# Delta head 0's three projection tiles and the gates' product on x*(1+scale), block by block, with W*shift added later

## The chip, the cores and the metric

The kernel runs on one core of a Trainium2 chip. The metric is the device time of one launch in microseconds (us); the median of 3 runs before the change is 921.39 us (920.76 to 921.51).

## What is computed

One inference step of a decoder layer, on 512 prompt tokens and 8 x 4 sample tokens (544 columns), all in float32:

```
shift, scale, gate = split(silu(c) @ w_cond + b_cond)     # 9 rows of c: one prompt, eight samples
h = x * (1 + scale) + shift
qa, ka, va, za, qkv_b, zb, a_b, b_b, g_a, g_b = h @ w_in  # 11,280 columns
branch A: dilated window attention, 24 heads of 64, with caches for the samples
branch B: gated DeltaNet, 8 heads of 128: short causal convolution (width 4) and silu on q, k, v,
          gates from a_b and b_b, chunked delta rule, RMSNorm, times silu(zb)
merged = sigmoid(g_a) * (yA @ w_branch_a) + sigmoid(g_b) * (yB @ w_branch_b)
y = LayerNorm(ALPHA * x + gate * (merged @ w_out))
```

The samples' updated caches are outputs too: they are copied from DRAM to DRAM, 512 KB at a time, all through the kernel.

## The kernel before

Everything on the chip is transposed: a tile has 128 features on the partitions and the 544 tokens along the free dimension. A float32 product is made of three products of rounded halves: a weight tile `wt` is split into `hi` (ScalarE copies it to the shorter format) and `lo` (VectorE subtracts), and h into `hhi` and `hlo`, and each of the 8 contraction steps k takes `hi*hhi`, `hi*hlo` and `lo*hhi`. One projection tile (128 output columns of w_in) is thus 2 halves of 272 tokens x 8 steps x 3 = 48 matmuls of 272 columns, written to PSUM tiles `pp`. 88 such tiles follow each other ("the stream"), and beside them run, on TensorE too, the small matmuls of attention (`pg`), of the delta blocks (`pb`) and of the delta rule (`pd`).

The order of instructions on each engine is fixed when the program is built. `body` records every operation with a rank, and `Recorder.schedule` is a list planner with assumed costs: it emits, engine by engine, the operation of lowest rank that it believes ready. All records therefore carry the same source line (L724 before, L723 after), and tiles are told apart by name. Some operations have a planned time (`at`): the cache copies and the loads of the gate third of w_cond.

The front, before the stream can start:

- `cT` (c transposed) is loaded, silu gives `cs`, 8 x 32 columns.
- The scale third of w_cond, then the shift third, come in four pieces `wc` of 1,024 KB each (two k steps, all 1024 columns). `cond_product` multiplies them: 16 matmuls of 32 rows by 512 columns for each third, four of them side by side in the array's four column strips. The four strips are summed and transposed back by eight small matmuls against `selc` (a part of the constants `cst`): `Y` is the copy out of PSUM, `pd<-cst,Y` the matmuls. Out of this come `sc` = 1 + scale and then `sh` = shift.
- `xT` (x transposed, 8 steps of 544 columns, 2.2 MB in all) becomes h: the samples' columns by `xs * sc` and `xs + sh` (VectorE), the prompt's by one `tensor_scalar` with sc and sh for each k (VectorE), then `hhi` (ScalarE) and `hlo` (VectorE) for each k.
- All transfers go through one queue, SyncE's (SPq).

The stream's first three tiles are q, k and v of delta head 0 (`conv_job(0, s)`, s = 1, 0, 2); next come nine attention tiles, six tiles of heads 1 and 2, and so on. A conv tile's `evac` copies PSUM to `ext` (ScalarE), a convolution of four steps follows (`acc`, one on ScalarE and three on VectorE), and silu into `KQ` or `uv`. `gates()` makes a product of 16 columns of w_in (`wab`, as `hl` with both halves in 32 columns) with hhi and hlo: 32 matmuls `pg<-hhi,hi 32x272`; its result `abT` goes through eight small matmuls and some 40 small VectorE operations on 34 columns, to `beta`, `cum` and, by DRAM, `drows`. `delta_blocks(h)` waits for KQ and the gates, transposes (`pb<-cst,KQ`), takes row norms (`rc`), sends them through DRAM (`dr`) and back as a broadcast (`rb`), scales KQ and multiplies (`pb<-KQ`). `gate_rows` makes the gate third, planned for 110 to 200 us.

Of the kernel before, what the change touches and what calls it, by code (L numbers as in the profile page):

```python
# [11 lines left out]
F32 = mybir.dt.float32  # L12
F32R = mybir.dt.float32r
# [232 lines left out]
class Recorder:  # L246
# [208 lines left out]
    def schedule(self):  # L455
# [37 lines left out]
        def ready(op):  # L493
# [283 lines left out]
def body(ctx, tc, io):  # L777
# [98 lines left out]
    wab = consts.tile([128, KT, 16], F32, name="wab")  # L876
    gctx = ExitStack()
    d1 = pool(gctx, "gtab", 1)
    tables["g"] = d1.tile([128, CONST[1].shape[1]], F32, name="cg")
    dta = d1.tile([128, 2, 34], F32, name="dta")  # L880
    with ExitStack() as fctx:
        fr = pool(fctx, "front", 1)
        cT = fr.tile([128, KT, 32], F32, name="cT")
        ve.memset(cT, 0.0)
        sp.dma_start(cT[:, :, 0:9], io["cT"])
        bT = fr.tile([128, 24], F32, name="bT")
        sp.dma_start(bT, io["bT"])
        th = fr.tile([128, KT, 32], F32, name="th")
        se.activation(th, cT, AF.Tanh, scale=0.5)
        ve.tensor_scalar(th, th, 0.5, 0.5, op0=OP.mult, op1=OP.add)  # L890
        ve.tensor_mul(cs, cT, th)
        xT = fr.tile([128, KT, NT], F32, name="xT")
        pieces = {}
        for part in (1, 0):
            for k in range(0, KT, 2):
                pieces[part, k] = fr.tile([128, 2, D], F32, name="wc", bufs=8)
                sp.dma_start(pieces[part, k], cond_rows(part, k, 2))
                if (part, k) == (1, 6):
                    sp.dma_start(cst, io["const"])
        sp.dma_start(wab, io["w_ab"])  # L900
        raws[0] = wraw.tile([128, D], F32, name="wt", tag="wraw")
        sp.dma_start(raws[0], io["w_in"][TILE_AT["b", 0, 1]])
        weights[0] = split(raws[0], D, ve)
        for k in range(0, KT, 2):
            sp.dma_start(xT[:, k:k + 2], io["xT"][:, k:k + 2])
# [4 lines left out]
        def load_front(part):  # L910
            for k in range(0, KT, 2):
                for n in range(2):
                    for q in range(2):
                        yield k + q, n, pieces[part, k][:, q, 512 * n:512 * n + 512]

        sc = fr.tile([128, KT, 9], F32, name="sc")
        sh = fr.tile([128, KT, 9], F32, name="sh")
        for part, t in ((1, sc), (0, sh)):
            ps = [pp(), pp()]
            take(cond_product(part, load_front, ps), 99)  # L920
            pv = f16(pd())
            bias = bT[:, 8 * part:8 * part + 8, None].to_broadcast([128, 8, 9])
            for n in range(2):
                Y = fr.tile([128, 512], F32, name="Y", bufs=2)
                if n:
                    se.activation(Y, ps[n], AF.Copy)
                else:
                    ve.tensor_copy(Y, ps[n])
                to_features(pv, 4 * n, Y)
            if part:  # L930
                ve.scalar_tensor_tensor(t, pv[:, :, 0:9], 1.0, bias, op0=OP.add, op1=OP.add)
            else:
                ve.tensor_add(t, pv[:, :, 0:9], bias)
        sp.dma_start(bnw, io["b_norm_w"])
        ve.tensor_scalar(hbnw, bnw, 0.5, None, op0=OP.mult)
        xs = xT[:, :, SEQ:].rearrange("p k (b t) -> p k b t", t=4)
        per_token = lambda t, k, n: t[:, k:k + n, 1:9, None].to_broadcast([128, n, 8, 4])
        for k in range(0, KT, 2):
            ve.tensor_mul(xs[:, k:k + 2], xs[:, k:k + 2], per_token(sc, k, 2))
        for k in range(0, KT, 2):  # L940
            ve.tensor_add(xs[:, k:k + 2], xs[:, k:k + 2], per_token(sh, k, 2))
        for k in range(KT):
            h = xT[:, k]
            ve.tensor_scalar(h[:, :SEQ], h[:, :SEQ], sc[:, k, 0:1], sh[:, k, 0:1], op0=OP.mult, op1=OP.add)
            se.activation(hhi[:, k, :], h, AF.Copy)
            ve.tensor_sub(hlo[:, k, :], h, hhi[:, k, :].bitcast(F32))
# [65 lines left out]

    two_tiles = lambda t: t[:, 0:512].rearrange("p (s g n) -> p s g n", s=2, g=2)
# [23 lines left out]
    def gates():  # L1037
        d1 = pool(gctx, "gt", 1)


        hl = cols128(wsp.tile([128, D], F32R, name="hi", tag="hi"))
        se.activation(hl[:, :, 0:16], wab, AF.Copy)
        ve.tensor_sub(hl[:, :, 16:32], wab, hl[:, :, 0:16].bitcast(F32))
        ps = [pg(), pg()]
        for n in range(2):
            for k in range(KT):
                for x in (hhi, hlo):
                    pe.matmul(ps[n][0:32, :HF], hl[:, k, 0:32], x[:, k, n * HF:(n + 1) * HF],
# [1318 lines left out]
```

## Time and profile before

| What | Value |
|---|---|
| Median of 3 runs | 921.39 us |
| Time of the profiled execution | 921.47 us |
| Its span, first to last instruction | 919.7 us |
| TensorE (PE) busy | 883.6 us, 96% of the span |
| VectorE (DVE), ScalarE (ACT), GpSimd (POOL) busy | 663.6, 459.5, 68.5 us |
| Moved by DMA | 240.09 MB, mean 261 GB/s |
| Mean granted TensorE clock | 0.987 |

Times in the profile count from the start of the span. A matmul's record includes the time that it takes to drain, so matmuls overlap in the records: what a stream of them costs is read from the distance of their starts, or from how many start in a stretch. A float32 matmul that isn't split by the kernel shows as two records. In the page's row of the granted clock, a digit is tenths of the full clock; the trace has an event only where the clock changes.

### The profile page before, as it was taken

The page shows a single profiled execution, that of the slowest core. Times are in us where ns is not written, and L with a number is a line of the kernel's source. Part 1 is how long each engine was busy: PE and PEld are TensorE (multiplying, and loading weights), DVE is VectorE, ACT ScalarE, POOL GpSimd, SP SyncE. Part 2 cuts the span into 40 slices and gives each one's busy share as a digit, 9 for nine tenths or more (in the row PEclk, how much of TensorE's full clock was granted, in tenths as well). Part 3 has the DMA queues.
Part 4 walks back from the last instruction along what each step waited for, and adds up shares of the span by engine and source line. Part 5 has one row for each costly group of instructions (what it writes and reads, how often), then busy time and mean ns, then how long its engine had stood idle before and what let it go on. Part 6 is the DMA issues. An engine that isn't in the chain of part 4 may idle for free.

```text
span 919.7 us, 20682 instructions
## 1 busy us (share of the span) xinstructions
PE 883.6 (96%) x8082; PEld 823.5 (90%) x8082; DVE 663.6 (72%) x1399; ACT 459.5 (50%) x1115; POOL 68.5 (7%) x186
## 2 busy tenths in 40 slices
PE   4899999999999999999999999999999999989995
PEld 1699998898999999898999989999999999989884
DVE  0574535674568999759999865656889799988578
ACT  0266457663568863577764676554342222224331
POOL 0120000100001200001200010002010000001000
PEclk9899999999999999999999999999999999999998
DMA  9778785765788879896889865648969899985933
GB/s 354 256 186 273 204 286 198 252 215 173 229 265 292 289 219 346 256 288 220 297 269 310 261 207 179 234 149 285 353 197 352 303 380 427 373 308 194 324 118 122
DMA packets 107807, 240.09 MB, mean 261 GB/s; under 512 B 31110, under 2 KB 62480, under 8 KB 105020
## 3 DMA queue, kind: packets, MB, share of 16 engines
q1 hardware_dynamic: 107708, 238.76, 77.4%
q8 instruction: 64, 1.05, 0.5%
q14 instruction: 35, 0.29, 0.1%
HBM read 222.40 MB, written 104.00 MB: 355 GB/s over the span
## 4 chain that ended last, share of the span: by engine, by line
PE 86%; DVE 5%; DMA 4%; ACT 2%; SPq 1%; issue 1%; DVEq 0%; POOL 0%; POOLq 0%; ACTq 0%
PE pp L724 67%; PE pg L724 8%; PE pd L724 7%; PE pb L724 4%; DMA rb<-dr 2%; DMA wc<-in_w_cond 1%; SPq L724 1%; DMA dO<-orow 1%; DVE r L724 1%; DVE acc L724 1%; DVE lo L724 1%; DVE xT L724 0%; ACT sq L724 0%; ACT hi L724 0%; DVE KQ L724 0%
## 5 line engine op out<-in xcount | busy, mean ns | idle before, releaser
L724 PE MATMUL pp<-hhi,hi 128*128 128x272 f32 x1408 | 416.4, 296 | 2.6 <-ACT hhi L724 2.1
L724 PE MATMUL pp<-hhi,lo 128*128 128x272 f32 x1408 | 417.1, 297 | 0.0
L724 PE MATMUL pp<-hlo,hi 128*128 128x272 f32 x1408 | 414.3, 295 | 0.4 <-DVE hlo L724 0.2
L724 PEld LDWEIGHTS pp<-hhi,hi 128*128 128x128 f32 x1408 | 266.7, 190 | 6.8 <-issue 2.9
L724 PEld LDWEIGHTS pp<-hhi,lo 128*128 128x128 f32 x1408 | 266.7, 190 | 3.7 <-issue 2.1
L724 PEld LDWEIGHTS pp<-hlo,hi 128*128 128x128 f32 x1408 | 266.7, 190 | 3.4 <-issue 1.4
L724 ACT ACTIVATE hi<-wt 128x1024 fp32r<-128x1024 f32 (+1 forms) x104 | 106.8, 1026 | 148.6 <-PE pp L724 111.7
L724 DVE TENSOR_TENSOR lo<-wt,hi 128x1024 fp32r<-128x1024 f32 (+1 forms) x104 | 122.6, 1179 | 72.7 <-ACT hi L724 72.3
L724 DVE SCALAR_TENSOR_TENSOR acc<-ext,cw,acc 128x568 f32<-128x568 f32 x72 | 57.4, 797 | 0.7 <-ACT acc L724 0.4
L724 ACT ACT_TABLE_LOAD x36 | 46.2, 1283 | 15.9 <-DMA cT<-in_cT 8.2
L724 DVE TENSOR_TENSOR slab<-slab 128x512 f32<-128x512 f32 (+1 forms) x66 | 42.9, 670 | 1.5 <-DMA slab<-in_ks 0.7
L724 DVE TENSOR_REDUCE slab<-slab 128x8 f32<-128x512 f32 (+2 forms) x66 | 42.5, 660 | 0.3
L724 ACT ACTIVATE zt<-pp 128x272 f32<-128x272 f32 x48 | 18.6, 388 | 42.9 <-PE pp L724 40.6
L724 PE MATMUL pp<-ybl,hi 128*128 128x272 f32 x128 | 36.9, 288 | 0.0
L724 PE MATMUL pp<-ybh,hi 128*128 128x272 f32 x128 | 36.9, 288 | 0.0
L724 PE MATMUL pp<-ybh,lo 128*128 128x272 f32 x128 | 36.9, 288 | 0.0
L724 ACT ACTIVATE P<-P,st 128x256 f32<-128x256 f32 (+1 forms) x64 | 31.3, 491 | 10.0 <-DVE st L724 9.8
L724 DVE CUSTOM_DVE_ANT_0 P<-pg,bias 128x256 f32<-128x256 f32 (+1 forms) x64 | 23.1, 401 | 15.2 <-PE pg L724 15.2
L724 POOL COPY cx<-ext 128x3 f32<-128x3 f32 (+1 forms) x48 | 24.7, 544 | 94.7 <-ACT ext L724 94.7
L724 DVE TENSOR_TENSOR Tb<-Tb,tmp 32x15 f32<-32x15 f32 (+7 forms) x120 | 23.4, 195 | 4.1
L724 ACT ACTIVATE ext<-pp 128x272 f32<-128x272 f32 (+2 forms) x72 | 19.9, 315 | 12.7 <-PE pp L724 12.7
L724 PE MATMUL pp<-wc,cs 128*32 128x512 f32 x64 | 13.7, 984 | 12.7 <-DMA wc<-in_w_cond 12.7
(382 smaller groups left out, 1527.5 us busy)
## 6 DMA issues: line engine op xcount, KB each, us to landing
out_kv_s<-in_cache SPq DMA_DIRECT2D x144, 512.0 KB
wt<-in_w_in SPq DMA_DIRECT2D x88, 512.0 KB
out_kv_s<-in_cache SPq DMA_DIRECT2D x24, 496.0 KB
wc<-in_w_cond SPq DMA_DIRECT2D x8, 1024.0 KB
slab<-in_ks SPq DMA_DIRECT2D x32, 256.0 KB
slab<-in_vs SPq DMA_DIRECT2D x32, 256.0 KB
kv<-in_ks SPq DMA_DIRECT2D x16, 512.0 KB
kv<-in_vs SPq DMA_DIRECT2D x16, 512.0 KB
```

The costliest lines, as they stand in the source:

```text
L724: getattr(real[x.engine], x.name)(*map(arg, x.args), **{k: arg(v) for k, v in x.kw.items()})
```

## The change

- w_cond's scale and shift thirds are laid out anew (`w_cb`): four blocks of 256 columns for each third, all 8 k steps in a block (two transfers of 512 KB). `cond_block` does for one block what the front did for a third: 8 matmuls of 32 x 256, a copy `Y`, two transposing matmuls.
- As soon as block b of scale is there, `x1` = x * sc is made for the two k steps 2b and 2b+1, in halves `x1h` (`x1[0]`, ScalarE) and `x1l` (`x1[1]`, VectorE), and these two steps of head 0's three tiles run on it: six PSUM tiles (`sums`, two each of the pools pp, pd, pg) stay open over all four blocks. Their weights and the gates' 16 columns are one new input, `w3` (tile `W3`, 400 columns, four loads of 410 KB). The gates' product also runs on x1.
- The six sums are copied to `raw` tiles and abT, without the shift. Shift's four blocks follow; then `W3 * sh` (8 matmuls 32 x 400 and four transposing ones) gives `shifts`, which `shifted()` adds (VectorE) when it fills `ext`, in place of ScalarE's evac.
- h itself is made block by block as shift lands; the `tensor_scalar` of odd k moves to GpSimd. The program that is built has one more GpSimd instruction ahead of them (a reload of its code library).
- cg, dta, abT, the raw tiles and the gates' small tiles lie in the nine tiles of the pool `op` (tag "o"), freed when the gates are done; `gate_rows` now waits for `gates_over` first. The gates have rank -2 in place of 2.
- In the planner, an operation waits for the free time of every tile that it touches, not of those alone that it is first to use. With that, rows move by a few places all through the program.

```diff
-                if t.ops[0] == op.n:
-                    r = max(r, t.free + self.WAKE[op.engine])
+                r = max(r, t.free + self.WAKE[op.engine])
...
+        def load_cond(part, b):
+            pieces[part, b] = fr.tile([128, KT, 256], F32, name="wc", bufs=4)
+            for k in (0, 4):
+                sp.dma_start(pieces[part, b][:, k:k + 4], io["w_cb"][part, b, :, k:k + 4])
...
+        for b in range(4):
+            load_cond(1, b)
+            if not b:
+                sp.dma_start(cst, io["const"])
+                sp.dma_start(bT, io["bT"])
+            sp.dma_start(xT[:, 2 * b:2 * b + 2], io["xT"][:, 2 * b:2 * b + 2])
+            sp.dma_start(W3[:, 2 * b:2 * b + 2], io["w3"][:, 2 * b:2 * b + 2])
+        for b in range(4):
+            load_cond(0, b)
+        for i in range(2):
+            raws[i] = wraw.tile([128, D], F32, name="wt", tag="wraw")
+            sp.dma_start(raws[i], io["w_in"][TILE_AT["a", 0, 0, i]])
...
+            with rec.together():
+                for k in range(KT):
+                    q = k % 4
+                    pe.matmul(ps[32 * q:32 * q + 32, 0:256], cs[:, k, :], wc[:, k, :], start=(k < 4), stop=(k >= 4),
+                              tile_position=(0, 32 * q))
+            Y = fr.tile([128, 256], F32, name="Y", bufs=2)
+            ve.tensor_copy(Y, ps[:, 0:256])
...
+            for k in range(2 * b, 2 * b + 2):
+                se.activation(x1[0][:, k, :SEQ], xT[:, k, :SEQ], AF.Copy, scale=sc[:, k, 0:1])
...
+                for t in range(3):
+                    w, w_ = (x[:, k % 2, 128 * t:128 * t + 128] for x in (hi, lo))
+                    for n in range(2):
+                        for a, x in ((w, 0), (w, 1), (w_, 0)):
+                            pe.matmul(sums[t][n], a, x1[x][:, k, cols_of(n)], start=(k == 0 and a is w and x == 0),
+                                      stop=(k == KT - 1 and a is w_))
...
+                pe.matmul(ps[32 * q:32 * q + 32, 0:400], sh[:, k, :], W3[:, k, :], start=(k < 4), stop=(k >= 4),
+                          tile_position=(0, 32 * q))
...
+        for b in range(4):
+            kk = slice(2 * b, 2 * b + 2)
+            ve.tensor_add(xs[:, kk], xs[:, kk], per_token(sh, 2 * b, 2))
+            for k in range(2 * b, 2 * b + 2):
+                h = xT[:, k]
+                (ge if k % 2 else ve).tensor_scalar(h[:, :SEQ], h[:, :SEQ], sc[:, k, 0:1], sh[:, k, 0:1], op0=OP.mult, op1=OP.add)
+                se.activation(hhi[:, k, :], h, AF.Copy)
+                ve.tensor_sub(hlo[:, k, :], h, hhi[:, k, :].bitcast(F32))
...
-    for s in (1, 0, 2):
-        jobs.append(conv_job(0, s))
+    for t, s in enumerate((1, 0, 2)):
+        job = conv_job(0, s)
+        job.begin()
+        job.shifted(first[t], shifts[:, t])
...
-    ab = threads.add(gates(), 2)
-    threads.add(stream(60 + 4 + EARLY_B), 9)
-    threads.run(lambda: ab["over"])
-    gctx.close()
+    threads.add(gates(), -2)
+    threads.add(stream(57 + 4 + EARLY_B), 9)
```

How rows move: a row names engine operation, output tile, input tiles and shape; in these lists the tile `W3` reads W_117 and the copy `Y4` reads Y_578. First TensorE at the start of the program. Before:

```order
L724 MATMUL pp<-wc,cs 32x512 x16
L724 MATMUL pd<-cst,Y 128x9 x8
L724 MATMUL pp<-wc,cs 32x512 x16
L724 MATMUL pd<-cst,Y 128x9 x8
L724 MATMUL pp<-hhi,hi 128x272 x2
```

After the change, TensorE at scale's block 2 (blocks 0 and 1 stand ahead of it in the same way):

```order
L723 MATMUL pg<-x1h,hi 128x272
L723 MATMUL pg<-wc,cs 32x256 x8
L723 MATMUL pg<-x1l,hi 128x272
L723 MATMUL pg<-x1h,lo 128x272
L723 MATMUL pp<-x1h,hi 128x272
L723 MATMUL pp<-x1l,hi 128x272
L723 MATMUL pp<-x1h,lo 128x272
```

Where both thirds of w_cond stood ahead of the first projection matmul, a block's product now stands among the tile matmuls of the blocks before it, and its two transposing matmuls some seven matmuls further on, here behind five on `pp`.

Second, TensorE where the front ends. Before, the gates' product on h begins behind the 42nd matmul of the first tile:

```order
L724 MATMUL pp<-hhi,hi 128x272
L724 MATMUL pp<-hlo,hi 128x272
L724 MATMUL pp<-hhi,lo 128x272
L724 MATMUL pg<-hhi,hi 32x272
L724 MATMUL pg<-hlo,hi 32x272
```

After, behind all 144 tile matmuls, three matmuls of the first attention tile and shift's last block, the gates' product on x1 ends and the shift's product stands inside it; these are its last rows:

```order
L723 MATMUL pg<-x1h,hl 32x272
L723 MATMUL pg<-x1l,hl 32x272
L723 MATMUL pp<-hhi,hi 128x272
L723 MATMUL pb<-cst,Y_578 128x9 x3
L723 MATMUL pb<-cst,Y_578 16x9
L723 MATMUL pp<-hlo,hi 128x272
L723 MATMUL pp<-hhi,lo 128x272
```

The stream on hhi and hlo thus goes on at the first attention tile, with head 0's three tiles and the gates' product behind it.

Third, VectorE at shift. Before (three more rows of the samples' columns and the eight `hlo` follow):

```order
L724 TENSOR_TENSOR sh<-pd,bT 128x72
L724 TENSOR_TENSOR xT<-xT,sh 128x2x32
L724 TENSOR_TENSOR xT<-xT,sc 128x2x32
L724 TENSOR_TENSOR xT<-xT,sh 128x2x32 x2
L724 TENSOR_SCALAR xT<-xT,sc,sh 128x512 x3
```

After, from shift's block 0 into block 1:

```order
L723 TENSOR_TENSOR sh<-pg,bT 128x2x9
L723 TENSOR_TENSOR xT<-xT,sh 128x2x32
L723 TENSOR_SCALAR xT<-xT,sc,sh 128x512
L723 COPY Y<-pb 128x256
L723 TENSOR_TENSOR hlo<-xT,hhi 128x544
L723 TENSOR_TENSOR sh<-pb,bT 128x2x9
L723 TENSOR_TENSOR lo<-wt,hi 128x1024
```

One `sh` for all k steps has become one for two of them, and each block's copy `Y`, for which TensorE waits, stands between subtractions `hlo` of the block before, which wait for ScalarE's hhi and for GpSimd's `tensor_scalar` of the odd k.

More of the change, by code (lines that the diff above doesn't have):

```diff
@@ new lines, in body @@
+    n = CONST[1].shape[1]
+    tables["g"] = early_[:, 0:n]
+    dta = early_[:, n:n + 68].rearrange("p (a b) -> p a b", b=34)
+    shifts = early_[:, n + 68:n + 104].rearrange("p (a b) -> p a b", b=9)
+    first = [op.tile([128, NT], F32, name="raw", tag="o") for _ in range(3)]
+    abT = op.tile([128, NT], F32, name="abT", tag="o")[0:32]
+    xs = xT[:, :, SEQ:].rearrange("p k (b t) -> p k b t", t=4)
+    per_token = lambda t, k, n: t[:, k:k + n, 1:9, None].to_broadcast([128, n, 8, 4])
+    cols_of = lambda n: slice(n * HF, (n + 1) * HF)
@@ L881, in body @@
     with ExitStack() as fctx:
         fr = pool(fctx, "front", 1)
-        cT = fr.tile([128, KT, 32], F32, name="cT")
-        ve.memset(cT, 0.0)
-        sp.dma_start(cT[:, :, 0:9], io["cT"])
+        cT = fr.tile([128, KT, 9], F32, name="cT")
+        sp.dma_start(cT, io["cT"])
         bT = fr.tile([128, 24], F32, name="bT")
[L887 to L890, printed above, removed]
@@ L934, in body @@
-        sp.dma_start(bnw, io["b_norm_w"])
-        ve.tensor_scalar(hbnw, bnw, 0.5, None, op0=OP.mult)
[L936 to L946, printed above, removed]
+        sp.dma_start(bnw, io["b_norm_w"])
@@ new lines, in body, with cond_block @@
+        ve.memset(cs, 0.0)
+        ge.memset(sh, 0.0)
+        th = fr.tile([128, KT, 9], F32, name="th")
+        se.activation(th, cT, AF.Tanh, scale=0.5)
+        ve.tensor_scalar(th, th, 0.5, 0.5, op0=OP.mult, op1=OP.add)
+        ve.tensor_mul(cs[:, :, 0:9], cT, th)
+        def cond_block(part, b):
+            ps, wc = pb_() if b % 2 else pg(), pieces[part, b]
+            rec.rank = -1
+            with rec.together():
[5 more added lines that the diff above has]
+            ve.tensor_copy(Y, ps[:, 0:256])
+            pv = ps[:, 256:288].rearrange("p (a b) -> p a b", b=16)
+            with rec.together():
+                for i in range(2):
+                    pe.matmul(pv[:, i, 0:9], Y[:, 128 * i:128 * i + 128], C("selc"), start=True, stop=True)
+            rec.rank = 0
+            return pv[:, :, 0:9], bT[:, 8 * part + 2 * b:8 * part + 2 * b + 2, None].to_broadcast([128, 2, 9])
@@ new lines, in body @@
+        Y = fx.tile([128, 400], F32, name="Y4")
+        rec.either(Y, ps[:, 0:400])
+        with rec.together():
+            for t in range(4):
+                m = 128 if t < 3 else 16
+                pe.matmul(pv[0:m, 16 * t:16 * t + 9], Y[:, 128 * t:128 * t + m], C("selc"), start=True, stop=True)
+        ve.tensor_copy(shifts[:, 0:3], pv[:, 0:48].rearrange("p (a b) -> p a b", b=16)[:, :, 0:9])
+        ve.tensor_copy(shifts[0:16, 3], pv[0:16, 48:57])
+        ab = abT[0:16]
+        ve.tensor_scalar(ab[:, :SEQ], ab[:, :SEQ], shifts[0:16, 3, 0:1], None, op0=OP.add)
@@ L1037, in gates, with tile @@
     def gates():
[L1038 to L1048, printed above, removed]
-                              start=(k == 0 and x is hhi), stop=(k == KT - 1 and x is hlo))
-        abT = d1.tile([32, NT], F32, name="abT")
-        for n in range(2):
-            se.activation(half(abT, n), ps[n][0:32, :HF], AF.Copy)
-        yield 2.0
+        packs, at = [], [NT]
+        spare_packs = [op.tile([128, NT], F32, name="gt", tag="o") for _ in range(3)]
+        class d1:
+            def tile(shape, dtype, name):
+                n = math.prod(shape[1:])
+                if at[0] + n > NT:
+                    packs.append(spare_packs.pop(0))
+                    at[0] = 0
+                t = packs[-1][0:shape[0], at[0]:at[0] + n]
+                at[0] += n
+                return t if len(shape) == 2 else t.rearrange("p (a b) -> p a b", b=shape[2])
         pa = pg()
```

140 lines of the change are left out of this document (83 added, 57 removed).

## The prediction

> **What bounds the kernel now.** The page first: busy times and the slices.
>
> ```profile
> PE 883.6 (96%) x8082; PEld 823.5 (90%) x8082; DVE 663.6 (72%) x1399; ACT 459.5 (50%) x1115; POOL 68.5 (7%) x186
> PE   4899999999999999999999999999999999989995
> ```
>
> TensorE (PE) is full from the third slice on and loses time only in the first two, 46 us. So I read that stretch next, in windows (after PE come granted clock, DMA share, GB/s):
>
> ```profile
> 10.00:20.00 10.00, 7.35 (x32) 1.00 1.03 407
> 20.00:30.00 10.00, 9.22 (x49) 1.00 1.03 407
> 30.00:40.00 10.00, 6.90 (x41) 0.66 0.92 305
> ...
> 90.00:100.00 10.00, 10.00 (x80) 1.00 0.68 189
> ```
>
> The last row is the steady stream: 80 matmuls in 10 us, 0.125 us each. From 10 to 30 us the DMA engines are full (407 GB/s) and PE does few matmuls. Which, and how fast, the timeline tells:
>
> ```profile
> 8.15 1.28 ACT L724 ACT_TABLE_LOAD   x1 [8.15 <-DMA cT<-in_cT]
> ...
> 10.85 1.93 PE L724 MATMUL pp<-wc,cs 128*32 128x512 f32 x8 [10.85 <-DMA wc<-in_w_cond]
> ...
> 18.45 1.94 PE L724 MATMUL pp<-wc,cs 128*32 128x512 f32 x8 [0.64 <-DMA wc<-in_w_cond]
> 21.16 3.58 PE L724 MATMUL pd<-cst,Y 128*128 128x9 f32 x16 [0.78 <-DVE Y L724]
> 24.68 5.92 PE L724 MATMUL pp<-wc,cs 128*32 128x512 f32 x32
> 31.40 2.39 PE L724 MATMUL pd<-cst,Y 128*128 128x9 f32 x16 [0.80 <-DVE Y L724]
> 35.92 0.82 PE L724 MATMUL pp<-hhi,hi 128*128 128x272 f32 x2 [2.13 <-ACT hhi L724]
> 37.31 0.43 PE L724 MATMUL pp<-hhi,lo 128*128 128x272 f32 x1
> 37.54 0.43 PE L724 MATMUL pp<-hhi,hi 128*128 128x272 f32 x1
> 157.15 1.92 PE L724 MATMUL pd<-wg,cs 128*32 128x512 f32 x16
> ```
>
> The front is two w_cond products, each behind its transfers, and no projection matmul before 35.9. Two more things stand here. The first piece of 1,024 KB is there at 10.85, the fourth at 18.45: 2.53 us each, the pace of the windows' 407 GB/s. And PE ran the front at half speed, whatever the window's clock column says before the first change of the clock: 8 records of the w_cond product took 1.93 us at 10.85, 16 equal ones 1.92 at 157.15; the stream at 37.5 started one matmul every 0.23 us, against 0.125 later. In the row at 24.68 32 records took 5.92 us: at 0.24 and 0.12 us each, the speed changed at about 28.8; the mean clock of 0.66 from 30 to 40 is half clock for 6.8 us of the ten.
>
> **Where the old front ends.** The chain of waits (start, us, what):
>
> ```profile
> 43.86 4.54 PE pg L724 x36
> 48.40 0.95 PE pp L724 x6
> 49.35 0.72 PE pg L724 x12
> 50.07 11.53 PE pp L724 x90
> 61.60 0.79 PE pg L724 x8
> 62.38 0.23 PE pp L724
> 62.61 1.19 PE pg L724 x10
> 63.80 1.46 PE pp L724 x10
> ```
>
> With the 42 tile matmuls ahead of 43.86 (the order above), the 144th of head 0's tiles is done five before the last row's end, at 64.6. In between PE did 32 matmuls of the gates' product and 3.2 us of other gate work (4 of the 36, then 0.72, 0.79, 1.19), which the change leaves behind the front. So before, "both w_cond products, 144 tile matmuls and 32 gate matmuls done" is at 64.6 - 3.2 = 61.4 us. The same point after the change gives the saving, if the stream behind it runs as before.
>
> **The change, part by part.** *Transfers.* At that pace, byte count B (in MB) lands at 18.45 + (B - 5.85)/0.407 us: 5.85 MB (xT's first part, two wt, cT, bT, four wc) are there at 18.45. After, one wt (0.52), cT, then block 0 come first: cT at 5.5 (so the table load, 1.28, ends at 6.8 and `cs` is ready at 7.6), block 0 of scale at 8.1, its x and W3 at 10.9, the next scale blocks at 13.4, 18.4, 23.4, the last W3 at 25.7, shift's blocks at 28.2, 30.8, 34.7 and 39.1. The two wt between them, for the first two attention tiles, land at 32.1 and 36.0, well before their use (51 and 57). Gate tables, passed by all this, land at 36.5; they are used at 54.
>
> *PE until it is fed.* Block 0's product runs at half speed, 8.1 to 10.0 (1.93), copy `Y` 0.4, two transposing matmuls (a quarter of 3.58) to 11.4. Then sc, and x1: W3 lands at 10.9, its `hi` (three quarters of 1.06) ends at 11.85, and the first x1h of 512 columns at about 12.65.
>
> ```profile
> L724 DVE TENSOR_TENSOR lo<-wt,hi 128x1024 fp32r<-128x1024 f32 x11 | 13.5, 1224 | 23.1 <-ACT hi L724 23.0
> L724 DVE TENSOR_TENSOR hlo<-xT,hhi 128x544 fp32r<-128x544 f32 x8 | 5.4, 714 | 0.7 <-ACT hhi L724 0.7
> L724 DVE TENSOR_SCALAR xT<-xT,sc,sh 128x512 f32<-128x512 f32 x8 | 3.9, 536 | 0.0
> L724 DVE COPY Y<-pp 128x512 f32<-128x512 f32 x2 | 1.4, 692 | 10.4 <-PE pp L724 10.4
> ...
> L724 ACT ACTIVATE hi<-wt 128x1024 fp32r<-128x1024 f32 x11 | 11.6, 1058 | 12.6 <-PE pp L724 11.0 <-PE pg L724 1.6
> L724 ACT ACTIVATE hhi<-xT 128x544 fp32r<-128x544 f32 x8 | 4.7, 648 | 6.8 <-DVE xT L724 6.8
> ...
> L724 POOL COPY cx<-ext 128x3 f32<-128x3 f32 x3 | 2.5, 849 | 7.9 <-ACT ext L724 7.9
> ...
> L724 POOL MEMSET XF<- 128x512 f32 x1 | 0.5, 525 | 0.0
> ```
>
> *PE from 12.65 on.* A scale block brings 36 tile matmuls (4.5 us), a product and two transposes, some 6 us; its data take 5 us to land and VectorE 3.5 us to prepare. PE has a backlog from here, so work adds up:
> - 176 tile and gate matmuls x 0.125 = 22.0;
> - 7 products: 16 records of 256 columns, half of 157.15's 1.92, plus 0.15 for the change of shape = 1.1 each, 7.7;
> - 7 pairs of transposes: 4 records, a quarter of 2.39 at most, 0.5 each, 3.5;
> - the shift's product, new: 16 records of 400 columns, 400/512 of 1.92 = 1.5, and 4 transposes, 0.95;
> - half speed at the start. Between 1.7 (half of the 3.4 us that the dense stream from 35.9 ran slowly) and 8.1 (half of 12.65 to 28.8). PE is as dense here as in the stretch from 35.9, the nearest case, but with gaps for block 0's x1l: 2.5;
> - waits: VectorE's `Y` of shift's last block stands behind `lo` of a weight tile (1.22) and hlo; PE reaches its transposes some 0.7 early, and W*shift 0.4 early: 1.1.
>
> Sum: 12.65 + 22.0 + 7.7 + 3.5 + 2.45 + 2.5 + 1.1 = 51.9 us. Saving 61.4 - 51.9 = 9.5 us.
>
> The Trainium skill, TensorE: Matmul & The Clock Gate, Part 1, has half speed end after one busy window of about 3.4 us; the trace agrees (0.23 us at 37.5, full clock 3.4 us behind 35.9). By it the fifth term would be 1.7, and the sum 51.1.
>
> *Work off PE.* h follows shift's blocks: the last `sh` at 47.8, hhi and hlo of k = 7 at 50.7, used behind 20 attention matmuls at about 54: covered by 3 us. GpSimd's `tensor_scalar` has no row; bounds are 0.53 (the memset of equal size) and 1.5 (three of them, since it reads, computes and may share VectorE's time); I take 1.0, nearest the memset. What queues behind it: hlo of odd k on VectorE, then the next block's `Y`, for which PE waits; PE's slack there is 1 us, so the upper end costs 0.5. The reload ahead of it stands on an idle engine at 1 us, first use at 34.6: between 0 and the 1.28 of ScalarE's table load, taken as 0. ScalarE's nine evac copies give way to six `raw` copies; VectorE gains three times one tensor_scalar and an add, 2.3 us, while PE streams.
>
> *Head 0's delta blocks* come later in the stream than before by some 75 matmuls, since ext now waits for `shifts` (51.9); on the clock they stay where they were (transposes at 62, against 65.3). Nothing before h = 1's third tile waits for them. `gate_rows`' wait ends at about 75, its work is planned from 110: nothing.
>
> *The planner's line* moves rows everywhere at equal counts. What it can gain or lose are later waits, and these are few:
>
> ```profile
> PE pb L724 <- DVE KQ L724: 4.5, 3, 2.2
> ```
>
> And a window behind the first of them:
>
> ```profile
> 179.40:182.80 3.40, 3.25 (x11) 0.52 0.62 238
> ```
>
> Two waits of 2.2 us for a scaled KQ (heads 1 and 2, behind the broadcast `rb`), each followed by 3.4 us at half clock (11 matmuls where the steady stream has 27): 3.9 us each. Bounds -7.8 (both gone) and +7.8 (two more); I take 0, as the number of matmuls between norms and KQ stays about the same (98 before and 101 after for head 1).
>
> So: 921.47 - 9.5 = 912.0 us by the profiled execution, whose span is 1.8 us under its time; the median is 0.08 lower. I say 912.
>
> **Rivals.**
> - *The KQ waits go too* (0.15): for head 2 the matmuls between norms and KQ rise from 94 to 133, and the transfers in front of `rb` move. 912 - 7.8 = 904; with one gone, 908.
> - *PE stays at half speed in the front* (0.11): before, products of 32 columns with gaps never raised the clock until 28.8. Then the term is 8.1 in place of 2.5: 918.
> - *GpSimd is late* (0.07): what it delivers late holds hlo of an odd k on VectorE, behind it the next block's `Y`, and so PE. If each of the four takes its upper bound and is held up beside VectorE as the copies `cx<-ext` seem to be (0.85 us for three columns), that is 4 x (0.5 + 0.75) = 5 us, less 1 of slack: 916. GPSIMD Engine Reference of the Trainium skill, section 2.1, gives about 6 us to the first call of freshly loaded code; no run here shows it, and as an estimate it would make the time 917 by the same queue.
> - *Given back* (0.08): the stream runs 9.5 us ahead of the same transfers and waits of the same chain, at other places; 2 to 3 more waits of 3.9 us: 921.
> - *Slower* (0.08): head 0's transposes. PE meets them, in its fixed order, at about 62, behind 80 attention matmuls. They need KQ, behind `shifts`, three convolution steps and some twenty gate operations on one VectorE queue, about 10.5 us from 51.9 on: 62.4. If the queue runs 9.5 us longer than that, to 72, the saving is gone; at 75, 924. Against it: VectorE's rows before did the same work in 50 to 65.
>
> **How the numbers follow.** The forecast (909 to 916) has the remaining 0.51. What differs from no change by less than 0.2%, 1.8 us, can't be told apart here. Faster: forecast, KQ, half speed and GpSimd, 0.84; within 0.2%: 0.07, most of "given back"; slower: 0.09. The range 903 to 919 holds the four faster cases.
>
> **What would show it.** Right: x1 matmuls from 12 to 13 us, the last on x1 at about 51, the first `cg,abT` at 54, PE without gaps over 1 us between 13 and 60; 0.125 us a matmul from some 18 us on. Wrong: starts 0.23 us apart beyond 25; a `tensor_scalar` on POOL that begins after 36; PE idle at `pb<-cst,KQ`; more waits on `rb` than two.

## The result, and the profile after

The changed kernel takes 905.75 us (median of 4 runs, 905.12 to 907.83; the profiled execution 906.21, its span 904.4). The kernel before, beside it, takes 921.14. The ratio is 0.9837, with a 95% interval of 0.982 to 0.9854: 15.4 us less. The forecast was 912, with 903 to 919 as its range.

The page of the changed kernel first, TensorE's busy time and its 40 slices:

```profile
PE 876.3 (97%) x8170; PEld 819.8 (91%) x8170; DVE 670.3 (74%) x1430; ACT 469.4 (52%) x1126; POOL 75.5 (8%) x191
PE   5999999999999999999999999999999999999995
```

PE is full from the second slice on; before, the second slice was at 8. The windows of the first stretch (after PE and PEld come DVE, ACT and POOL busy, granted clock, DMA share, GB/s):

```profile
0.00:10.00 10.00, 1.30 (x12) 0.43 (x16) 0.89 (x6) 1.54 (x2) 0.51 (x5) 1.00 0.79 265
10.00:20.00 10.00, 7.79 (x51) 5.61 (x44) 4.54 (x10) 3.06 (x5) 0.00 (x0) 1.00 1.02 417
20.00:30.00 10.00, 10.00 (x95) 8.53 (x95) 5.90 (x15) 4.49 (x9) 0.00 (x0) 1.00 1.03 418
30.00:40.00 10.00, 10.00 (x95) 8.46 (x94) 6.75 (x15) 4.12 (x7) 2.15 (x2) 1.00 0.85 334
```

From 20 us on PE runs 95 records in 10 us, where before it ran 49 and 41. The DMA engines are as full as before, at 418 GB/s: the same transfers now have matmuls beside them. How the stretch starts, in the timeline (start us, busy us, engine, operation):

```profile
8.59 2.27 PE L723 MATMUL pg<-wc,cs 128*32 128x256 f32 x16 [8.59 <-DMA wc<-in_w_cb]
12.59 0.84 ACT L723 ACTIVATE hi<-W 128x768 fp32r<-128x768 f32 x1 [7.74 <-DMA W<-in_w]
14.10 0.59 PE L723 MATMUL pp<-x1h,hi 128*128 128x272 f32 x1 [1.67 <-ACT x1h L723]
16.89 1.65 PE L723 MATMUL pb<-wc,cs 128*32 128x256 f32 x16
21.99 1.07 PE L723 MATMUL pg<-wc,cs 128*32 128x256 f32 x16
```

And how it ends, in the chain of waits (start, us, what):

```profile
44.51 1.00 PE pb L723 x16
...
47.81 3.72 PE pg L723 x33
51.66 0.72 PE pb L723 x8
```

The first matmul on x1 starts at 14.10; it waits for x1h, which stands behind W3's `hi` on ScalarE, and that for W3's transfer. The product of the second block takes 1.65 us, that of the third, equal in work, 1.07: between them half speed has ended. The last row is the transposing of W*shift; with it the front ends at 52.4, against 61.4 before. That is 9.0 us by the prediction's count; on the stream itself the lead is 7.9 us where both kernels have the gates behind them (the tile that starts at 104 us in the kernel before). The rest, 6.4 us by the first count, comes far behind the front, where waits of PE are gone. The waits of PE over the whole span, before:

```profile
PE pb L724 <- DVE KQ L724: 4.5, 3, 2.2
...
PE pp L724 <- ACT yah L724: 2.1, 1, 2.1
```

and after (in total, times, longest; us):

```profile
PE pp L723 <- DVE spare L723: 1.4, 1, 1.4
...
PE pb L723 <- DVE KQ L723: 1.1, 2, 0.8
```

With each of these waits, half clock behind it is gone: from 65 us on, waits over 0.8 us and the time lost to half clock fall from 7.2 + 5.1 to 4.0 + 0 us. Before, the wait for `yah` at 823.8 is followed by a window at half clock, first row; in the changed kernel the same place, second row, is dense:

```profile
827.90:831.30 3.40, 3.38 (x15) 3.00 (x14) 1.91 (x3) 1.31 (x2) 0.00 (x0) 0.52 0.40 154
```

```profile
823.00:832.00 9.00, 9.00 (x73) 9.00 (x73) 8.16 (x16) 3.88 (x6) 1.82 (x3) 1.00 0.51 175
```

After the front, the changed kernel's clock stays at full speed to 898.7 us; before, it was halved three times, for 3.4 us each. (In both it is halved once more, some six us from the end.)

### The profile page after: what moved, and what is told of

Same layout as the page of the kernel before. It is cut to its first block, busy times and chain, and to the rows that moved or that the text cites. A ratio compares the mean times of both kernels' runs of the same rounds, so it can differ in the third digit from the quotient of the medians.

```text
span 904.4 us, 20926 instructions
## 1 busy us (share of the span) xinstructions
PE 876.3 (97%) x8170; PEld 819.8 (91%) x8170; DVE 670.3 (74%) x1430; ACT 469.4 (52%) x1126; POOL 75.5 (8%) x191
## 3 DMA queue, kind: packets, MB, share of 16 engines
q8 instruction: 64, 1.05, 0.5%
## 4 chain that ended last, share of the span: by engine, by line
PE 86%; DVE 5%; ACT 4%; DMA 3%; issue 1%; SPq 1%; POOL 0%; DVEq 0%; ACTq 0%; POOLq 0%
PE pp L723 64%; PE pg L723 9%; PE pd L723 8%; PE pb L723 4%; DVE acc L723 1%; DMA W<-in_w 1%; DMA dO<-orow 1%; ACT L723 1%; DVE r L723 1%; DMA Ls<-dblk 1%; SPq L723 1%; DVE lo L723 1%; ACT P L723 1%; ACT sq L723 1%; DMA stc<-in_state_conv 0%
## 5 line engine op out<-in xcount | busy, mean ns | idle before, releaser
L723 PE MATMUL pp<-hhi,hi 128*128 128x272 f32 x1360 | 400.3, 294 | 2.3 <-DVE spare L723 1.4
L723 PE MATMUL pp<-hhi,lo 128*128 128x272 f32 x1360 | 400.9, 295 | 1.2 <-DVE lo L723 1.2
L723 PE MATMUL pp<-hlo,hi 128*128 128x272 f32 x1360 | 401.0, 295 | 0.0
L723 PEld LDWEIGHTS pp<-hhi,hi 128*128 128x128 f32 x1360 | 256.4, 188 | 5.7 <-issue 2.0
L723 PEld LDWEIGHTS pp<-hlo,hi 128*128 128x128 f32 x1360 | 256.5, 189 | 4.5 <-issue 3.1
L723 PEld LDWEIGHTS pp<-hhi,lo 128*128 128x128 f32 x1360 | 256.2, 188 | 4.4 <-issue 1.5
L723 ACT ACTIVATE hi<-wt 128x1024 fp32r<-128x1024 f32 (+1 forms) x101 | 103.6, 1026 | 135.9 <-PE pp L723 114.2
L723 DVE TENSOR_TENSOR lo<-wt,hi 128x1024 fp32r<-128x1024 f32 (+1 forms) x101 | 119.0, 1178 | 73.2 <-ACT hi L723 71.8
L723 ACT ACTIVATE zt<-pp 128x272 f32<-128x272 f32 x48 | 18.7, 390 | 46.2 <-PE pp L723 44.9
L723 POOL COPY cx<-ext 128x3 f32<-128x3 f32 (+1 forms) x48 | 23.4, 515 | 100.3 <-ACT ext L723 97.6
L723 DVE TENSOR_TENSOR tmp<-Ls,Tb 32x15 f32<-32x15 f32 (+7 forms) x120 | 23.2, 193 | 4.9 <-DMA Ls<-dblk 1.6
L723 DVE TENSOR_TENSOR Tb<-Tb,tmp 32x15 f32<-32x15 f32 (+7 forms) x120 | 23.4, 195 | 4.1
L723 ACT ACTIVATE spare<-pp 128x272 f32<-128x272 f32 (+1 forms) x32 | 16.1, 503 | 16.5 <-PE pp L723 16.3
```

The source lines that it names most:

```text
L723: getattr(real[x.engine], x.name)(*map(arg, x.args), **{k: arg(v) for k, v in x.kw.items()})
```

## The experiments

The open question was the 6.4 us. All runs stand beside runs of the kernel before on the same chip (medians 919.8 to 920.8), and the ratios are to these. "Lead" below is how much earlier than in the kernel before a stream tile starts, tile by tile (48 matmuls into pp each, counted in the records of the trace; head 0's three tiles are left out of the count where they run on x1).

**The two halves of the change alone.** The change consists of the new front and of one line of the planner. The first kernel has the new front with the old line, the second the old front with the new line:

```diff
             for t in op.tiles:
-                r = max(r, t.free + self.WAKE[op.engine])
+                if t.ops[0] == op.n:
+                    r = max(r, t.free + self.WAKE[op.engine])
```

> The change without its line in the planner: the front alone. Theory A (the front gives some 9 us, and the planner's line the 6 us that came later, by taking away the two waits for KQ and the half-clock stretches behind them): the shift's last transposes end at 52 as in the changed kernel, two waits of about 2 us at pb<-KQ stand there again, 912 us. Theory B (the 6 us come from the front too: whatever moves the rows moves the waits): no or one wait of 2 us, 904 to 909 us.

> The kernel before with the planner's line alone. Theory A: the old front (144th tile matmul at 64.6), but no wait of 2 us at KQ and no half clock after 40 us: 915 us. Theory B: the line by itself gives nothing that lasts; the waits of 2 us are there at these or other places: 919 to 923 us.

Front alone: 916.32 us (10 runs, 913.47 to 922.83), ratio 0.9964 (0.9938 to 0.9989). Line alone: 917.21 (10 runs, 914.73 to 921.66), ratio 0.9972 (0.9953 to 0.9992). Each is worth about 4 us, and together 8, not 15. Neither pair of theories fits: the front alone has no wait for KQ over 1.0 us and is still slower than both had it; the line alone lies between its two, and one wait for KQ, 2.6 us at 178, is left. Yet the front of the first is as good as the changed kernel's: last x1 matmul at 51.0, lead 18.1 us at 511.6 us. Then it falls to 3.5 within 36 us, and it is 6.6 at 626. What happens there, in the timeline and in windows of this kernel:

```profile
514.05 1.27 DVE L724 TENSOR_TENSOR slab<-slab 128x512 f32<-128x512 f32 x2
...
516.43 0.33 DVE L724 SCALAR_TENSOR_TENSOR z<-pd,necum,vr 128x128 f32<-128x128 f32 x1
516.82 0.80 PE L724 MATMUL pd<-z,XF 128*128 128x128 f32 x2 [2.16 <-DVE z L724]
```

```profile
500.00:510.00 10.00, 9.61 (x77) 9.23 (x75) 9.38 (x31) 3.45 (x8) 0.40 (x2) 1.00 0.98 355
510.00:530.00 20.00, 14.09 (x155) 10.55 (x155) 17.61 (x33) 13.02 (x36) 2.87 (x9) 0.74 0.80 282
```

VectorE is busy 27.0 of 30 us. It works on the cache's `slab` when PE needs `z`, PE stands 2.16 us and then a string of smaller waits, and the clock is halved for 10.2 us. Neither half of the change has work of its own there, so I put it down to the place of a few rows in the order; no run moves these rows alone.

**Block by block or whole.** This kernel gathers the scale of all four blocks before any x1:

```diff
-            ve.scalar_tensor_tensor(sc[:, kk], pv, 1.0, bias, op0=OP.add, op1=OP.add)
+            ve.scalar_tensor_tensor(sc_[:, kk], pv, 1.0, bias, op0=OP.add, op1=OP.add)
+        ve.tensor_copy(sc, sc_)
+        for b in range(4):
+            kk = slice(2 * b, 2 * b + 2)
             for k in range(2 * b, 2 * b + 2):
                 se.activation(x1[0]...
```

> The changed kernel, but x1 is made only when all four blocks of scale are there (one more copy of 72 columns ahead of it): no tile matmul between the blocks. Theory (PE is the bound from the time it is fed, and what the front gains is the time by which it is fed earlier): x1 begins at about 26.5 in place of 13.3, then 176 matmuls 22, four products and pairs 6.4, the shift's product 2.45, waits and half clock 3: the shift's last transposes end at about 60 in place of 52.4, 913 us. Rival (the front ends where shift's last block lands, 39 us, and its chain behind it): ends at 52.4 to 54, 906 to 908 us.

It takes 929.16 us (928.13 to 931.96), ratio 1.011 (1.0079 to 1.0141). In its timeline the first x1 matmul starts at 28.66:

```profile
28.66 0.60 PE L723 MATMUL pp<-x1h,hi 128*128 128x272 f32 x1 [1.41 <-ACT x1h L723]
```

and the last at 62.4, 11.2 us behind the changed kernel's. The front's gain is thus the matmuls that run while w_cond lands; with the same arithmetic and without them, this front is no earlier than the one before. The time is 16 us above the theory's 913, though: 23.4 us above the changed kernel, of which the front has 11.2. Behind the front this kernel, planned anew, has other waits (14.5 us against 4.0) and three stretches of half clock, so its time says nothing of the front alone.

**The half speed at the start, planned anew.** 20 matmuls of ones ahead of the first product and 12 behind it keep PE busy from 1.05 us on:

```diff
+        for i in range(WARM[0]):
+            pe.matmul(warm[:, 0:128], ones, ones, start=True, stop=True)
```

> The changed kernel with 20 float32 matmuls of 128 columns on a constant ahead of the first product and 12 behind it, in time in which PE idles; their result isn't used. Theory (half speed at the start costs the front about 2 us: 14.1 to 18.2 at half rate): the first x1 matmuls start 0.125 apart in place of 0.23, the shift's last transposes end at about 50.3, 904 us. Rival (transfers or VectorE hold the front, PE's speed there is hidden): 52.4 and 906 us as before.

916.6 us (10 runs, 915.09 to 920.23), ratio 0.9968 (0.9951 to 0.9986). The clock is full from 6.8 us, the front ends 2.0 us earlier, the lead is 14.1 at 665.6 us and 6.0 at 687.8. A better front, and 11 us slower than the changed kernel, where theory and rival had 904 and 906: with the added rows the planner puts the later rows in another order.

**The same with the order kept.** To separate the two, this kernel keeps the changed kernel's rows on every engine and puts the matmuls of ones between them:

```diff
+        warm(turned[1] + 1, seq[products[8]][1].outs[0].base, WARM[1])
+        warm(products[0], seq[products[0]][1].outs[0].base, WARM[0])
...
         rec.schedule()
+        rec.revise()
```

> The changed kernel with its planned order kept row for row on every engine; only 20 fp32 128x128 matmuls of ones by ones stand ahead of the first w_cond product and 12 behind block 0's transposes, so that TensorE is busy from about 4.6 us on. Theory A (the time after the front is fixed by which rows stand behind which; a gain in the front goes through to the end when the rows stay as they are): the clock is full from about 7, the front ends 2 us earlier (50.3 against 52.4), and the time falls by the same 2 us, to 903.7 (902.8 to 904.6). Theory B (later waits for transfers and VectorE set the end and give back what the front gains, as in the warm-up kernel that was planned anew, 916.6): the front ends 2 us earlier but the time stays within 0.7 of 905.75, or is above it.

907.03 us (905.42 to 909.12), ratio 0.9855 (0.983 to 0.988): no gain, as theory B had it. Here the trace shows the place. The lead over the changed kernel is 2.07 us at every tile from 76 to 116 us, 1.9 at 347, and -0.1 at 363. The chain of waits of this kernel there:

```profile
340.50 7.34 DMA rb<-dr
347.86 1.24 DVE KQ L742
349.14 1.13 PE pb L742 x4
```

and SyncE's queue ahead of it, in this kernel and then in the changed one:

```profile
333.30 0.30 SPq L742 DMA_DIRECT2D dr<-rrow  x1
333.65 5.19 SPq L742 DMA_DIRECT2D wv<-dw  x5
...
340.50 0.58 SPq L742 DMA_DIRECT2D rb<-dr  x1
```

```profile
335.21 0.30 SPq L723 DMA_DIRECT2D dr<-rrow  x1
335.56 3.02 SPq L723 DMA_DIRECT2D wv<-dw  x5
...
340.57 0.59 SPq L723 DMA_DIRECT2D rb<-dr  x1
```

The transfer `dr`, from which the broadcast `rb` reads, is still issued 1.9 us earlier than in the changed kernel. Between it and `rb` stand five transfers `wv` in the same queue; here three of them wait until older transfers (`wt`, twice `slab`) have landed, so they take 5.19 us in place of 3.02, and the next transfer waits for a cache copy until 339.6 (338.9 in the changed kernel). `rb` is issued at 340.5 in both and here takes 7.3 us, so KQ is no earlier than before. PE came 2 us earlier and waited. The lead is lost in SyncE's queue, at transfers that wait for older ones.

**And the first transfer moved.** As the last kernel, with 14 and 14 matmuls of ones in place of 20 and 12, and with the 512 KB of the first stream weight, first in SyncE's queue, put behind block 0 of W3:

```diff
+        i = at(lambda x: x.name == "dma_start" and "wt" in names(x))
+        row = seq.pop(i)
+        seq.insert(at(lambda x: x.name == "dma_start" and "W3" in names(x)) + 1, row)
```

> As the kernel with the kept order and warm-up matmuls (14 ahead and 14 behind), and one more row moved: the 512 KB transfer of the first stream weight, first in the SyncE queue in the changed kernel, stands behind block 0 of W3. Theory A: block 0 and W3 land 1.3 us earlier (512 KB at about 390 GB/s), the first x1 matmul starts at about 12.0 to 12.8 (14.1 in the changed kernel), the front ends at about 49.2, and the time is 902.4 (901.2 to 903.5). Theory B (order of transfers is not what holds the first x1 matmul, it is the scale's chain Y, transposes, x1h): first x1 matmul as in the kernel without the moved row, and the same time as that one within 0.4.

904.7 us (903.51 to 905.3), ratio 0.9827 (0.9804 to 0.985), the fastest kernel of all. Its first x1 matmul is 2.2 us earlier than the changed kernel's, and here `rb` is issued earlier too:

```profile
11.86 0.37 PE L746 MATMUL pp<-x1h,hi 128*128 128x272 f32 x1
```

```profile
338.80 0.58 SPq L746 DMA_DIRECT2D rb<-dr  x1
```

Of a lead of 2.5 us behind the front 1.1 is left at the end. The front gained only 0.5 us on the last kernel's, where theory A had 1.3: PE, fed earlier, now waits 1.2 us at 18.7 for the second transfer of a later block. The time is 2.3 us below the last kernel's, and all five runs lie below its five, so theory B is out; theory A's range, to 903.5, is missed too. In the traces the gain on the last kernel is 0.5 us behind the front, 1.3 at 347 us and 2.4 at 355, where `rb` is, and 1.5 at the end. As the matmuls of ones differ too, it is not shown that the transfer's place alone makes it. The interval of the ratio overlaps that of the changed kernel. Against the kernel of the next paragraph, whose order is the changed kernel's in all but four rows, the 5 runs all lie below the 4 there.

**GpSimd.** The order kept, the four operations of h that run on GpSimd put on VectorE:

```diff
+            if kind == "op" and x.engine == "ge" and x.name == "tensor_scalar":
+                x.engine = "ve"
```

> The changed kernel with its order kept row for row; only the four scale-and-shift operations of x that run on GpSimd (0.83 to 2.26 us each in its trace) run on VectorE in the same places (0.54 each). Theory A (they lie beside the x1 matmuls and hold nobody): the same time, 905.75 within 0.6, and head 0's first rows on hhi start at the same 52.4. Theory B (the 1.0 us that the prediction put into the sum for GpSimd's slower row is on the path): 904.7, and the first hhi matmul 1 us earlier. Theory C (VectorE has no room there): 906.5 to 908, the x1 matmuls wait for x1l.

906.05 us (906.03 to 906.99), ratio 0.9845 (0.982 to 0.9871): no difference in the time, as theory A had it; the front ends at 52.1 in place of 52.4. The GpSimd rows of the changed kernel, two of four:

```profile
36.23 0.83 POOL L723 TENSOR_SCALAR xT<-xT,sc,sh 128x512 f32<-128x512 f32 x1 [35.19 <-DVE xT L723]
38.68 2.26 POOL L723 TENSOR_SCALAR xT<-xT,sc,sh 128x512 f32<-128x512 f32 x1 [1.62 <-DVE sh L723]
```

One took 2.26 us, beyond the upper bound of 1.5, and still cost at most 0.3 us of the front. The run also says how well this order repeats when it is kept: 906.05 against 905.75.

**Other orders of the same work.** Two constants of the planner were moved by 0.03 us, from 70 us on, so that the front's rows stay and the rest is put in another order:

```diff
-                    r = max(r, p.end + (self.AGAIN[op.engine] if data else 0.0))
+                    r = max(r, p.end + (self.AGAIN[op.engine] + 0.03 * (p.end > 70.0) if data else 0.0))
```

```diff
-                    r = max(r, p.done + self.WAKE[op.engine] + self.margin(p, op) if data else p.end)
+                    r = max(r, p.done + self.WAKE[op.engine] + self.margin(p, op) + 0.03 * (p.done > 70.0) if data else p.end)
```

> The changed kernel, planned with one constant moved: from 70 us on, the planner thinks that an operation that uses the result of the one ahead of it on the same engine starts 0.03 us later. The front's rows are the same, the work is the same, the rows behind stand in a somewhat different order. Theory A (the place of single waits and of the 3.4 us at half clock behind them is chance of the order): front ends at 52.4, and the time is anywhere from 905 to 918, most likely near 912, the sum of the prediction. Theory B (the changed planner line itself keeps the later waits away): within 1.5 us of 905.75.

> The kernel before, planned with the same constant moved (from 70 us on, an operation that uses the result of the one ahead of it on the same engine is thought to start 0.03 us later). Its front is the old one, the 144th tile matmul at about 64. Theory A (the front's 9 us reach the end on the average, and chance of the order adds to both kernels alike; the changed kernel so nudged took 917.7): 921 to 932, most likely 926. Theory B (later waits give most of the front's 9 us back, whatever the order; the changed kernel's 905.75 is one lucky order): 916 to 921, near the nudged changed kernel.

> The kernel before, planned with another constant moved: from 70 us on, a result is thought to reach another engine 0.03 us later. Theory A: 921 to 932, most likely 926. Theory B: 914 to 921.

> The changed kernel, planned with that second constant moved in the same way. Front as in the changed kernel (52.4). Theory A (chance of the order, 905 to 918 as so far): most likely 914, and 6 to 12 us below the kernel before nudged in the same way. Theory B (given back later): 914 to 918 and within 4 us of the kernel before nudged in the same way.

Results: changed kernel 917.72 (916.02 to 921.92), ratio 0.9971 (0.9952 to 0.999), by the first nudge, 911.52 (910.49 to 913.3), 0.9903 (0.9882 to 0.9923), by the second; kernel before 913.11 (912.8 to 913.44), 0.9918 (0.9901 to 0.9935), and 915.38 (914.37 to 918.4), 0.9953 (0.9936 to 0.997). By the first nudge the new front is slower by 4.6 us, by the second faster by 3.9. All orders together, old fronts first:

| kernel | front's last matmul, us | lead at 384 us | last delta step `pd<-S,KQ` at, us | lead at 681 us | waits over 0.8 us, sum | half clock, us | time, us |
|---|---|---|---|---|---|---|---|
| before | 64.3 | 0 | 619.7 | 0 | 7.2 | 10.2 | 921.1 |
| planner's line alone | 63.7 | 5.9 | 615.8 | 7.0 | 6.3 | 3.4 | 917.2 |
| before, nudge 1 | 63.9 | 7.8 | 615.4 | 8.1 | 5.5 | 0 | 913.1 |
| before, nudge 2 | 64.9 | 8.1 | 616.1 | 5.2 | 6.8 | 3.4 | 915.4 |
| changed | 51.2 | 14.3 | 605.8 | 13.0 | 4.0 | 0 | 905.75 |
| new front, old line | 51.0 | 15.5 | 616.1 | 6.2 | 12.8 | 13.7 | 916.3 |
| changed, nudge 1 | 51.5 | 16.8 | 621.0 | 5.8 | 17.2 | 10.2 | 917.7 |
| changed, nudge 2 | 52.1 | 13.4 | 613.5 | 6.8 | 6.6 | 10.2 | 911.5 |

(All points are starts in the profile. The front's last matmul is the 144th tile matmul with an old front, the last on x1 with a new one, so the two are not the same point. The leads are counted to the kernel before: at 384 us from the start of a tile, at 681 from the last matmuls of one. Waits and half clock count from 65 us on, without the half clock of the last ten us; a wait is the time between the starts of two matmuls.)

Each new front has an old one beside it that is planned alike: the two unnudged with the old line, the two unnudged with the new line, and the two nudged pairs (there the new front has the new line, the old one the old). At 104 us the new fronts lead these partners by 7.3 to 9.6 us, 8.0 on the average: the front's saving is there in all four. At 384 us the average is 15.0 - 5.45 = 9.5, from 5.3 to 15.5. At 681 us it is 8.0 - 5.1 = 2.9, from -2.3 to 6.2, and the times differ by 916.7 - 912.8 = 3.9, from -4.6 to 11.5. Four pairs that scatter so can't say how much is left in general (the 95% interval of the 3.9 goes from about -7 to 14); they do say that one order loses all of it, while in another the time falls by more than the front's saving.

Between the two points lie the last delta blocks and the samples' state. There the last delta step comes 2.7 us earlier on the average (616.8 against 614.1), though PE's stream came 9.5 us earlier at 384. Theory B, that later waits give most of it back whatever the order, is nearer to these averages, but its ranges hold for one of the two kernels before (915.4) and not for the other (913.1, below 916); theory A's 926 for both was wrong by 13 and 11 us. The changed kernel by the second nudge lies below theory B's range and within its 4 us of its partner. The changed kernel itself is the one new front that kept its lead, and the kernel before the slowest of the old ones. A fifth order of the new front, that of the matmuls of ones planned anew, took 916.6.

A wait over 1 us for a KQ of heads 1 and 2 stands in none of the four new fronts; in the old ones there are two, one, one and none.

**Moving the rows that make a wait.** In the first nudged changed kernel PE waits for VectorE's `zt` at 625.7 and 662.9. In its order, else kept, ScalarE's Tanh rows and VectorE's zt rows at these places were put ahead of a weight's split (rows of the order, at the first place):

```diff
-ACTIVATE hi<-wt 128x1024
 ACTIVATE zt<-pp 128x272 x2
+ACTIVATE hi<-wt 128x1024
```

> The first nudged changed kernel (917.72), with its order kept row for row but for a handful of rows at two places where TensorE waits for a PSUM bank (2.9 us at 625.7 and 3.3 us at 662.9, each followed by 3.4 us at half clock): there ScalarE's two Tanh rows that empty the bank stand ahead of the split of a stream weight (hi, 1.06 us), and VectorE's two zt rows ahead of lo (1.2 us; at the second place ahead of one ybl too). Theory A (single rows in an unlucky place and the half clock behind them make the loss): the first wait falls below 0.8 us and its half clock goes (2.6 + 1.7), the second falls to about 1.6 (1.7, and 1.7 more if its half clock goes): 910.0 to 911.7. Theory B (the load of VectorE there is what counts, the wait comes back a few us later): 916 to 918.

919.98 us (10 runs, 918.31 to 924.5), ratio 1.0 (0.9984 to 1.0015): not faster, and the median is 2.3 us above that without the moves, past theory B's range too. PE's waits from 620 to 675 us, ahead of the move and with it:

```profile
PE pp L723 <- DVE zt L723: 5.6, 2, 3.0
```

```profile
PE pp L746 <- DVE zt L746: 2.5, 2, 2.3
PE pd L746 <- DVE ys L746: 1.6, 1, 1.6
PE pg L746 <- DMA rbo<-dO: 0.9, 1, 0.9
PE pb L746 <- DMA S<-in_state_delta: 0.7, 1, 0.7
```

The first wait went, which won 2.8 us by 636 us. By 684 the kernel had lost that and 0.5 more, to `zt` and `ys` in close succession, to two transfers and to 6.8 us of half clock in one piece. In the window from 660 to 670 us of the kernel ahead of the move VectorE was busy 9.19 of 10 us:

```profile
660.00:670.00 10.00, 7.01 (x48) 6.77 (x47) 9.19 (x16) 5.23 (x8) 2.32 (x6) 0.87 0.72 251
```

So theory A, that single rows make the loss, is out for these two places: with the rows moved, PE waits at others. That VectorE's load makes it is not shown: in the moved kernel the same window has VectorE at 7.45 of 10 us, and PE waits there too. How much of the giving back is VectorE's load, how much the serial chain of the delta steps and how much the transfers is not settled by these runs.

## Why the prediction was right, and where not

- *The front* was forecast to end at 51.9 and ended at 52.4; its saving was 9.0 in place of 9.5. That the sum came so close is in part luck, as its terms were off both ways. By the distances of starts it is 14.1 + 23.7 + 7.0 + 2.7 + 2.2 + 2.0 + 0.7 = 52.4, where the forecast had 12.65 + 22.0 + 7.7 + 3.5 + 2.45 + 2.5 and, for waits, 1.1. In this order:
  - PE was fed at 14.10 (+1.45), as W3 was there at 12.57 and not at 10.9. The pace is not the reason: by 10.85 us 2.99 MB had been moved, more than the 2.78 that the estimate needs. The trace marks the landing of a transfer's 16 parts one by one: of this one the first is there at 9.85, twelve by 10.65, the last at 12.57, and ScalarE waits for all.
  - The 176 tile and gate matmuls took 0.135 us each on the average, not 0.125: those beside a product, and those behind a pair, took 0.20 to 0.22.
  - A product took 1.00, not 1.1. The prediction has no row for the 0.15 for the change of shape, and no run shows it inside a product: that took 0.04 over half of 1.92. The change shows in the matmuls beside it, as said.
  - A pair took 0.38, not 0.5 (its records, 0.51, overlap the next matmul). W*shift and its transposes took 2.2, close to 2.45.
  - Half speed lasted 4.0 us, from 14.1 to 18.1, and cost half of that. (In the kernel before, the trace has full clock first from 29.3, not 28.8, and in the dense stream 3.65 us behind 35.9, not 3.4. Both make little difference to the bounds.)
  - No wait over 0.15 us stands between 14.1 and 52.4; four attention matmuls (0.7) ran inside the stretch instead.
- *The signs*: the last matmul on x1 came at 51.2 as forecast, the first at 14.1 and not from 12 to 13, the first `cg,abT` at 55.1, not 54. One sign of being wrong came true, a `tensor_scalar` on GpSimd that begins after 36 (36.23), and cost nothing that could be measured.
- *GpSimd*: taken at 1.0, bounds 0.53 to 1.5; measured 0.83, 2.26, 0.94 and 0.94. The bound was wrong and the cover held: with these rows on VectorE the time is the same. The first of them began as soon as its data were there. The Trainium skill, GPSIMD Engine Reference, section 2.1, has about 6 us for the first call of freshly loaded code; the trace shows none of it ahead of this row, whose engine had been idle for 35 us.
- *Head 0's transposes* met a wait of 0.8 us ahead of 64.3, not the ten of the rival on the slower side.
- *The planner's line*, under which the prediction put the later waits, is the term that failed: taken as 0 between -7.8 and +7.8. With the line alone the time fell by 3.6, and in the changed kernel both KQ waits and the wait for `yah` went with their half clock; with the smaller waits that came instead, 6.4 us net. So the outcome is that of the first rival, *the KQ waits go too* (0.15; 904 or 908), to which the forecast had given less than a third of its own chance. Those KQ waits are gone in every order with the new front, with the old line too, and with the line alone one of them stands; so they go with the front, as that rival had it, rather than with the line (though one order of the old front has none either). The wait for `yah` was in no term, though the same view listed it; it comes and goes with the order.
- The step behind this failure is the tacit one that "the stream behind it runs as before". On the average it does to 384 us. Behind that the saving meets other limits; in the kernel with kept order it was SyncE's queue ahead of `rb`, in the others the traces name VectorE, the delta chain and transfers without settling which. Over four orders each, 2.9 of 9.5 us are left at 681 us. That is the rival *given back* (0.08) in its mechanism, more waits with half clock behind them (the new fronts in other orders have 10.2 to 13.7 us of half clock), though none of them reached its 921. In the other orders tried, the new front took 911 to 918. The forecast of 912 lies near the mean of the four, 912.8, but not for the reason that it gave, and with orders that scatter by 12 us that is luck: that mean is the saving mostly given back, from a mean of 916.7 for the old front, of which the kernel before was the slowest.

## What to carry to other kernels

Where a planner sets the order, one kernel on each side compares two orders as much as two designs: plan both again with a constant moved by a hair, and compare means, over more orders than the four here where they scatter as much as the gain. A gain in one stage is followed to the end by the lead at fixed points of the bounding engine's stream; where the lead falls, the next limit stands, and pushing the front further (here by 2.1 and 2.5 us more, of which 0 and 1.1 were left) buys little there. To try a local edit by itself, keep the finished order and put the edit into it.

## What the runs showed of the hardware

- Behind the front nine traces have 19 waits of PE of 2.0 to 3.3 us. With 15 of them a stretch of half clock began, in the wait or up to 2.2 us behind its end, of 3.4 us or a multiple; one lay inside such a stretch; behind three (2.9, 3.0 and 3.3 us by the records) the clock stayed full. Of the waits between 1.6 and 1.9 us most left it full too: 1.86 us for KQ in the kernel with kept order did, 1.71 us for `yah` in the kernel with the planner's line alone did not. So 3.9 us for a wait of 2.2 is what it costs when the clock is caught, not each time. The Trainium skill, TensorE: Matmul & The Clock Gate, Part 1, speaks of a window of about 3.4 us that runs freely. The length agrees with the 3.4 us of the traces, and a window that runs freely would explain why equal waits end differently; these traces show a halved clock already behind waits shorter than that window.
- The broadcast `rb` (512 KB) took 7.3 us from its issue at 340.5 to landing in the kernel with kept order, with the DMA engines at a share of 1.00 from 340 to 350 us, and 6.7 in the one with the moved transfer. In the changed kernel, where PE came 2 us later, KQ began 7.0 us behind the issue and nobody waited.
- The 16 parts of one transfer can land far apart: those of W3's block 0 from 9.85 to 12.57 us, those of its x from 8.85 to 11.54.
- The changed kernel's order, which has no half clock between the front and the end, repeats within 0.3 us in the median (905.75 and 906.05), while the order alone moves the median of equal work by 8 us with the old front and by 12 with the new. Runs of one and the same kernel differ more where it has half clock: those of the front alone go from 913.5 to 922.8.
